# Storing the low parts of the projection weights in the first half of the sequence and loading them in the second

## The chip, the cores and the metric

The kernel runs on one core of a Trainium2 chip. The metric is the device time of one execution in microseconds (us). The engines are named as the profile names them: PE (TensorE, matrix products; PEld is its weight load), DVE (VectorE), ACT (ScalarE), POOL (GpSimd) and SP (SyncE, which here only issues DMAs; its instructions are listed as SPq). A DMA moves data between device memory and the on-chip memory.

## The reference

One layer of a decoder trunk over 1024 positions (`SEQ`) of 1024 channels (`D_MODEL`), all in float32:

```python
h = layer_norm(x, ln_in_g, ln_in_b)
u = h @ w_in            # conformer a, g | ssm z | ssm x, B, C | dt | gate_a | gate_b
y_a = silu(layer_norm(causal_dwconv31(a * sigmoid(g)))) @ w_conv_out
y_b = mamba2_ssd(z, x, B, C, dt) @ w_ssm_out      # conv4, chunks of 128, grouped RMS norm
mix = (sigmoid(gate_a) * y_a + sigmoid(gate_b) * y_b) @ w_o
h = layer_norm(2**0.25 * h + mix, ln1_g, ln1_b)
ffn = (silu(gate) * val) @ w_down  with  gate, val = split(causal_dwconv3(h @ w_up))
h = layer_norm(2**0.25 * h + ffn, ln2_g, ln2_b)
```

## The kernel before

**Halves.** The 1024 positions are worked in two halves of 512 (`hh` 0 and 1). Each half runs `ln_in` (norm and transpose), `mixers` (input projections, the state-space part in four groups, the 31-tap convolution) and `combine` (gates, `wssm`, `wconv`). Half 0 then runs `out_proj` with `wo`, half 1 `out_proj_pairs` inside `ffn_blocks`. The feed-forward part comes last, over all 1024 positions, from its own weights.

**Split products.** Every product is made of three matmuls (`mm3`, L166 to L168): a float32 operand is held as a high part in the fp32r type and a low part (what rounding left), and high·high, high·low and low·high are summed in PSUM. The helper `weights` makes the two parts of one weight tile of 128 x 1024: SP loads it into `st` (L152; three buffers), ACT casts it into `w[:, 0]` (L154), and DVE subtracts that from `st` into `w[:, 1]` (L155; for the first three tiles of half 0 POOL does it). `w` has three buffers too. The input projections, `wssm`, `wconv` and `wo` pass through it in both halves, from the same weights: `out_proj_pairs` reads each of the eight `wo` tiles twice, once for each pair of 128-position blocks.

**How long a tile lasts.** In most places one weight tile feeds 24 matmuls of 512 columns. In `out_proj_pairs` (L695) it feeds 12, since one pair of blocks is worked at a time.

**Order.** A scheduler orders each engine's instructions by a simulated time; `high_priority` moves the weight loads ahead. Each engine then runs its list in order. A DMA that waits for something on SP keeps all later DMAs of SP waiting. SP's DMAs also go round eight semaphores, so that one waits until the DMA eight before it has landed.

**Names around the change.** `st_c`, `st_z`, `st_ga`, `st_gg`, `st_so`, `st_gt`, `st_gb`, `st_sp`, `st_co`, `st_wo` are the staged weight tiles, `w_` the split ones; `c` is the accumulator of the 31-tap convolution (L420, on DVE); `x`, `in_g`, `in_b` are the rows and parameters of `ln_in`; `r`, `ln_g` (`ln1_g`), `ln_b` the rows and parameters of the norm behind `wo`; `h_scr`, `h1_scr`, `c_scr`, `g_scr`, `y_scr` are scratch in device memory.

Of the kernel before, what the change touches and what calls it, by code (L numbers as in the profile page):

```python
# [1 line left out]

# [6 lines left out]
F32 = mybir.dt.float32  # L9
# [7 lines left out]
P = 128  # L17
D = 1024
# [38 lines left out]
def kernel(  # L57
# [15 lines left out]
    V, A, G, TE, SY = nc.vector, nc.scalar, nc.gpsimd, nc.tensor, nc.sync  # L73
# [8 lines left out]
    dram = ctx.enter_context(tc.tile_pool(name="scr", bufs=1, space=DRAM))  # L82
# [5 lines left out]
    def bank(which):  # L88
        n_ps[0] += 1
        pl, tag = (pacc, "acc") if which else (psm, "sm")  # L90
        return pl.tile([P, 512], F32, tag=tag, name=f"{tag}{n_ps[0]}")
# [54 lines left out]
    g_scr = [dram.tile([8, P, HALF], F32, name=f"g_scr{i}") for i in range(2)]  # L146
    y_scr = [dram.tile([8, P, HALF], F32, name=f"y_scr{i}") for i in range(2)]

    def weights(src, name, pl=None, eng=None, bufs=None):
        with tc.high_priority(offset=4000):  # L150
            st = wst.tile([P, D], F32, tag="st", name=f"st_{name}")
            SY.dma_start(st, src)  # L152
            w = (pl or wsp).tile([P, 2, D], F32R, tag="w", bufs=bufs, name=f"w_{name}")
            A.copy(w[:, 0, :], st)  # L154
            (eng or V).tensor_tensor(  # L155
                out=w[:, 1, :], in0=st, in1=w[:, 0, :].bitcast(F32), op=ALU.subtract
            )
        return w

    def big_tile(name):  # L160
# [2 lines left out]
    def mm3(ps, wa, xa, start, stop, more=False):  # L163


        TE.matmul(ps, wa(0), xa(0), start=start, stop=False, skip_group_check=more)  # L166
        TE.matmul(ps, wa(0), xa(1), start=False, stop=False, skip_group_check=more)  # L167
        TE.matmul(ps, wa(1), xa(0), start=False, stop=stop, skip_group_check=more)  # L168
# [40 lines left out]
    def ln_stats(pl, tiles, name, sts=None):  # L209

        n = len(tiles)
        mv = pl.tile([P, n, 2], F32, tag="ln_mv", bufs=2, name=f"mv_{name}")
        rs = pl.tile([P, n], F32, tag="ln_rs", bufs=2, name=f"rs_{name}")
        for i, t in enumerate(tiles):
            if sts:
                st = sts[i]
            else:
                st = pl.tile([P, 2, 6], F32, tag="ln_st", bufs=2, name=f"st_{name}{i}")
                for q in range(2):
                    ln_part(pl, t, st, q)  # L220
            V.bn_aggr(out=mv[:, i, :], in_=st)
        A.activation(out=rs, in_=mv[:, :, 1], func=AF.Sqrt, bias=eps)
        V.reciprocal(out=rs, in_=rs)
        return mv, rs

    def ln_apply(t, mv, rs, i, g, b):
        V.scalar_tensor_tensor(
            out=t, in0=t, scalar=mv[:, i, 0:1], in1=g, op0=ALU.subtract, op1=ALU.mult
        )
        V.scalar_tensor_tensor(  # L230
            out=t, in0=t, scalar=rs[:, i : i + 1], in1=b, op0=ALU.mult, op1=ALU.add
        )
# [110 lines left out]
    def column(hh, hT, ct):  # L343
        ps = bank(1)
        project(ps, weights(wcol[ct], f"c{hh}_{ct}"), hT)
        return ps

    def first_columns(hh, hT, cts):

        ws = [weights(wcol[ct], f"c{hh}_{ct}", eng=None if hh else G) for ct in cts]  # L350
        pss = [bank(1) for _ in cts]
        for q in range(2):
            ts = slice(q * 256, (q + 1) * 256)
            for w, ps in zip(ws, pss):
                for n, (i, j) in enumerate(((0, 0), (1, 0), (0, 1))):
                    for k in range(KD):
                        TE.matmul(  # L357
                            ps[:, ts],
                            w[:, i, k * P : (k + 1) * P],
                            hT[:, j, k, ts],  # L360
                            start=n == 0 and k == 0,
                            stop=n == 2 and k == KD - 1,
                        )
        return pss
# [23 lines left out]
    def glu(pl, hh, hT, i):  # L388
        pa, pg = bank(1), bank(1)
        wa = weights(wcol[CT_A + i], f"ga{hh}_{i}")  # L390
        project(pa, wa, hT)
        wg = weights(wcol[CT_G + i], f"gg{hh}_{i}")
        project(pg, wg, hT)
        v = pl.tile([P, HALF + KC - 1], F32, tag="v", bufs=4, name=f"v{hh}_{i}")
        s = pl.tile([P, HALF], F32, tag="sig", name=f"sig{hh}_{i}")
        A.activation(out=s, in_=pg, func=AF.Sigmoid)
        A.copy(v[:, : KC - 1], v_halo[:, i, :])
        V.tensor_mul(v[:, KC - 1 :], pa, s)
        if hh == 0:
            A.copy(v_halo[:, i, :], v[:, HALF:])  # L400
        return v
# [293 lines left out]
    def out_proj_pairs(pl, rs, mixT, g, b, done):  # L695

        for t in range(4):
            SY.dma_start(rs[t], h_scr[1][t * P : (t + 1) * P, :])
        for pair in range(2):
            ts = (2 * pair, 2 * pair + 1)  # L700
            pss = {(t, q): bank(1) for t in ts for q in range(2)}
            for kp in range(4):
                for q in range(2):
                    w = weights(wo[q, kp], f"wo1_{pair}_{q}_{kp}")
                    for t in ts:
                        for k in range(2):
                            mm3(
                                pss[t, q],
                                lambda i: mixT[:, i, 2 * kp + k, t * P : (t + 1) * P],
                                lambda i: w[:, i, k * HALF : (k + 1) * HALF],  # L710
                                kp == 0 and k == 0,
                                kp == 3 and k == 1,
                            )
            for t in ts:
                for q in range(2):
                    r = rs[t][:, q * HALF : (q + 1) * HALF]
                    V.scalar_tensor_tensor(
                        out=r, in0=r, scalar=ALPHA, in1=pss[t, q], op0=ALU.mult, op1=ALU.add
                    )
            for t in ts:  # L720
                mv, rstd = ln_stats(pl, rs[t : t + 1], f"o1_{t}")
                ln_apply(rs[t], mv, rstd, 0, g, b)
                done(t)
# [20 lines left out]
    def ffn_blocks(tp, qp, mixT):  # L744
# [33 lines left out]
        def block_sums(t):  # L778
# [17 lines left out]
            if t >= 2:  # L796
# [5 lines left out]
                kept.clear()  # L802

        out_proj_pairs(tp, rest, mixT, g, b, block_sums)
        return {
            "b11": lambda i: b1[:, i, 0:4, :],
# [425 lines left out]
```

## Time and profile before

| | |
|---|---|
| median of 3 runs | 2033.85 us (2031.81 to 2035.5) |
| profiled execution: time, span | 2035.35 us, 2033.6 us |
| granted PE clock, mean | 0.991 |
| PE, DVE, ACT, POOL busy, share of the span | 97%, 84%, 49%, 8% |
| moved by DMA | 273.51 MB, mean 134 GB/s |
| device memory read, written | 222.36 MB, 49.55 MB |

The profile is one execution. Its time lies 1.75 us above its span. A row of the windows view gives, for a stretch of the span, the busy time of each engine with the number of its instructions, the granted PE clock (1.00 is full), the mean busy share of the 16 DMA engines, and what they moved in GB/s.

### The profile page before, as it was taken

What the parts mean: (1) busy time and instruction counts of PE and PEld (TensorE: products, weight loads), DVE (VectorE), ACT (ScalarE), POOL (GpSimd) and SP (SyncE); (2) the same over time, 40 slices, a digit from 0 to 9 for tenths busy, and PEclk for the clock granted to TensorE, in tenths of its full rate; (3) what the DMA queues carried; (4) which work ended last, traced back from release to release, by engine and by line L of the source; (5) the groups of instructions that cost most, each with busy time, mean ns of one, the idle gap of its engine ahead of it and who ended that gap; (6) DMA issues with size and microseconds to landing.
All of it is one profiled execution on the core that took longest, in us unless ns stands there. A gap on an engine that the chain in (4) does not pass through costs nothing.

```text
span 2033.6 us, 24571 instructions
## 1 busy us (share of the span) xinstructions
PE 1978.0 (97%) x9164; PEld 1628.0 (80%) x9164; DVE 1710.7 (84%) x2285; ACT 1001.8 (49%) x1448; POOL 171.9 (8%) x141
## 2 busy tenths in 40 slices
PE   6999999999999999999999999998899999989998
PEld 6888887888788888888888888887778888777886
DVE  7599999989766869999998976596998788777868
ACT  4465654556453356665454645364334445443432
POOL 2010101001400000100100130010000000010000
PEclk9999999999999999999999999999999999999999
DMA  6212233332546522222423354565342232377563
GB/s 219 93 63 94 79 102 106 99 104 101 174 133 216 195 88 77 88 85 75 127 86 107 109 166 138 188 234 202 130 153 106 99 109 99 109 258 264 175 224 109
DMA packets 97303, 273.51 MB, mean 134 GB/s; under 512 B 11168, under 2 KB 11168, under 8 KB 97184
## 3 DMA queue, kind: packets, MB, share of 16 engines
q1 hardware_dynamic: 87696, 242.06, 35.9%
q0 software_dynamic: 7184, 25.69, 3.3%
q10 hardware_dynamic: 2304, 4.20, 0.6%
q8 instruction: 72, 1.18, 0.2%
q14 instruction: 47, 0.39, 0.1%
HBM read 222.36 MB, written 49.55 MB: 134 GB/s over the span
## 4 chain that ended last, share of the span: by engine, by line
PE 66%; DVE 24%; DMA 4%; issue 4%; ACT 1%; SPq 0%; DVEq 0%; ACTq 0%
PE acc L166 17%; PE acc L168 17%; PE acc L167 17%; DVE c L420 8%; PE sm L166 3%; PE sm L167 3%; PE sm L168 3%; DVE xbc L375 2%; DMA dr<-b_scr 1%; PE acc L357 1%; PE sm L534 1%; DVE fo L895 1%; DMA st_wo<-wo 1%; PE sm L515 1%; DVE w_so L155 1%
## 5 line engine op out<-in xcount | busy, mean ns | idle before, releaser
L420 DVE SCALAR_TENSOR_TENSOR c<-v,pc,c 128x512 f32<-128x512 f32 x480 | 375.3, 805 | 7.6 <-ACT c L409 6.1
L478 POOL TENSOR_TENSOR au<-seg_mv,head_of 128x1024 fp32r<-128x1024 f32 x32 | 76.3, 2383 | 962.2 <-PE sm L487 730.4
L166 PE MATMUL acc<-hT,w_c 128*128 128x512 f32 x352 | 141.1, 401 | 0.0
L167 PE MATMUL acc<-hT,w_c 128*128 128x512 f32 x352 | 140.7, 400 | 0.0
L168 PE MATMUL acc<-hT,w_c 128*128 128x512 f32 x352 | 138.5, 393 | 0.0
L895 DVE SCALAR_TENSOR_TENSOR fo<-u,pc,fo 128x1024 f32<-128x1024 f32 x88 | 111.5, 1279 | 8.5 <-ACT fo L891 7.8
L375 DVE SCALAR_TENSOR_TENSOR xbc<-u,pc,xbc 128x512 f32<-128x512 f32 x144 | 109.7, 774 | 0.7 <-ACT xbc L373 0.5
L167 PE MATMUL acc<-w_z,hT 128*128 128x512 f32 x256 | 100.9, 394 | 0.0
L166 PE MATMUL acc<-w_z,hT 128*128 128x512 f32 x256 | 100.9, 401 | 0.0
L168 PE MATMUL acc<-w_z,hT 128*128 128x512 f32 x256 | 100.7, 396 | 0.0
L1021 ACT CAST w_dn<-dr 128x1024 fp32r<-128x1024 f32 (+1 forms) x73 | 60.8, 842 | 77.7 <-DVE dr L951 31.5
L154 ACT CAST w_c<-st_c 128x1024 fp32r<-128x1024 f32 x50 | 52.5, 1051 | 86.8 <-PE acc L168 66.1
L1022 DVE TENSOR_TENSOR w_dn<-dr,w_dn 128x1024 fp32r<-128x1024 f32 (+1 forms) x73 | 69.6, 963 | 17.6 <-ACT w_dn L1021 17.5
L167 PEld LDWEIGHTS acc<-hT,w_c 128*128 128x128 f32 x352 | 66.2, 188 | 16.8 <-issue 3.8
L168 PEld LDWEIGHTS acc<-hT,w_c 128*128 128x128 f32 x352 | 66.1, 188 | 16.0 <-issue 2.6
L166 PEld LDWEIGHTS acc<-hT,w_c 128*128 128x128 f32 x352 | 66.1, 188 | 15.9 <-issue 2.6
L155 DVE TENSOR_TENSOR w_c<-st_c,w_c 128x1024 fp32r<-128x1024 f32 x47 | 60.6, 1289 | 20.2 <-ACT w_c L154 20.2
L166 PE MATMUL acc<-h1s,w_s 128*128 128x512 f32 x168 | 66.6, 397 | 5.7 <-ACT u L875 5.7
L166 PE MATMUL acc<-h1b,w_ue 128*128 128x512 f32 x176 | 68.9, 392 | 2.6 <-ACT w_ue L740 1.4
L166 PE MATMUL sm<-h1b,w_s 128*128 128x512 f32 x176 | 70.3, 400 | 0.0
L167 PE MATMUL sm<-h1b,w_s 128*128 128x512 f32 x176 | 70.3, 399 | 0.0
L168 PE MATMUL sm<-h1b,w_s 128*128 128x512 f32 x176 | 69.9, 397 | 0.0
(352 smaller groups left out, 5811.1 us busy)
## 6 DMA issues: line engine op xcount, KB each, us to landing
st_c<-wcol SPq DMA_DIRECT2D x50, 512.0 KB, 3.5
st_z<-wz SPq DMA_DIRECT2D x32, 512.0 KB, 3.4
st_wo<-wo SPq DMA_DIRECT2D x24, 512.0 KB, 3.8
ra<-wup SPq DMA_DIRECT2D x22, 512.0 KB, 3.6
rb<-wup SPq DMA_DIRECT2D x22, 512.0 KB, 3.4
t_scr<-fo POOLq DMA_DIRECT2D x22, 512.0 KB, 4.2
dr<-t_scr SPq DMA_DIRECT2D x44, 256.0 KB, 3.4
dr<-wdown SPq DMA_DIRECT2D x38, 256.0 KB, 3.8
```

The source lines that it names most:

```text
L154: A.copy(w[:, 0, :], st)
L155: (eng or V).tensor_tensor(out=w[:, 1, :], in0=st, in1=w[:, 0, :].bitcast(F32), op=ALU.subtract)
L166: TE.matmul(ps, wa(0), xa(0), start=start, stop=False, skip_group_check=more)
L167: TE.matmul(ps, wa(0), xa(1), start=False, stop=False, skip_group_check=more)
L168: TE.matmul(ps, wa(1), xa(0), start=False, stop=stop, skip_group_check=more)
L357: TE.matmul(ps[:, ts], w[:, i, k * P : (k + 1) * P], hT[:, j, k, ts], start=n == 0 and k == 0, stop=n == 2 and k == KD - 1,)
L375: V.scalar_tensor_tensor(out=o, in0=u[:, k : k + HALF], scalar=pc[:, wc + k : wc + k + 1], in1=o, op0=ALU.mult, op1=ALU.add,)
L420: V.scalar_tensor_tensor(out=accs[i], in0=v[:, k : k + HALF], scalar=pc[:, wc + k : wc + k + 1], in1=accs[i], op0=ALU.mult, op1=ALU.add,)
L478: G.tensor_tensor(out=au, in0=seg_mv[:, c, :].unsqueeze(1).to_broadcast([P, 8, P]), in1=head_of[:, g, :].unsqueeze(2).to_broadcast([P, 8, P]),
L895: V.scalar_tensor_tensor(out=o, in0=u[:, k : k + T], scalar=pc[:, wc + k : wc + k + 1], in1=o, op0=ALU.mult, op1=ALU.add,)
L1021: A.copy(w[:, 0, cs], src)
L1022: V.tensor_tensor(out=w[:, 1, cs], in0=src, in1=w[:, 0, cs].bitcast(F32), op=ALU.subtract)
```

## The change

For each tile that `weights` makes in half 0 under a name with a 0 behind its letters (`c0_`, `ga0_`, `z0_`, `wo0_` and so on, 105 tiles), the low part is stored to device memory after it is made. For each such tile of half 1 (names with 1, and with 2 for the second pair of `out_proj_pairs`; 113 tiles) the low part is loaded into `w[:, 1]` in place of DVE's subtraction. ACT's cast and the load of `st` stay. All the new DMAs are issued by SP, 512 KB each.

```diff
+import re
...
+    low_scr = {}
+
     def weights(src, name, pl=None, eng=None, bufs=None):
+        half = re.match(r"([a-z]+)([012])_(.*)$", name)
+        key = half and (half.group(1), half.group(3))
         with tc.high_priority(offset=4000):
             st = wst.tile([P, D], F32, tag="st", name=f"st_{name}")
             SY.dma_start(st, src)
             w = (pl or wsp).tile([P, 2, D], F32R, tag="w", bufs=bufs, name=f"w_{name}")
+            if half and half.group(2) != "0" and key in low_scr:
+                SY.dma_start(w[:, 1, :].bitcast(F32), low_scr[key])
+                A.copy(w[:, 0, :], st)
+                return w
             A.copy(w[:, 0, :], st)
             (eng or V).tensor_tensor(
                 out=w[:, 1, :], in0=st, in1=w[:, 0, :].bitcast(F32), op=ALU.subtract
             )
+        if half and half.group(2) == "0":
+            low_scr[key] = dram.tile([P, D], F32, name=f"low_{name}")
+            SY.dma_start(low_scr[key], w[:, 1, :].bitcast(F32))
         return w
...
-                    w = weights(wo[q, kp], f"wo1_{pair}_{q}_{kp}")
+                    w = weights(wo[q, kp], f"wo{pair + 1}_{q}_{kp}")
```

The instruction lists show where the new DMAs stand. In a row, the name left of the arrow is written and the one right of it read. First SP's list at the start of `out_proj_pairs`, before:

```order
L152 DMA st_wo1_0_1_2_10548<-wo 128x1024
L203 DMA ln1_g_10370<-prow 128x1024
L203 DMA ln1_b_10372<-prow 128x1024
L750 DMA r0_10374<-h1_scr_125 128x1024
L750 DMA r1_10375<-h1_scr_125 128x1024
L152 DMA st_wo1_0_0_3_10565<-wo 128x1024
L750 DMA r2_10376<-h1_scr_125 128x1024
L152 DMA st_wo1_0_1_3_10582<-wo 128x1024
```

And SP's list at the same place after the change, where `low_wo0_q_kp` is the stored low part (L160 loads it):

```order
L157 DMA st_wo1_1_2_10758<-wo 128x1024
L160 DMA w_wo1_1_1_10726<-low_wo0_1_1_5649 128x1024
L215 DMA ln1_g_10580<-prow 128x1024
L215 DMA ln1_b_10582<-prow 128x1024
L157 DMA st_wo1_0_3_10775<-wo 128x1024
L762 DMA r0_10584<-h1_scr_125 128x1024
L762 DMA r1_10585<-h1_scr_125 128x1024
L160 DMA w_wo1_0_2_10743<-low_wo0_0_2_5544 128x1024
L762 DMA r2_10586<-h1_scr_125 128x1024
L157 DMA st_wo1_1_3_10792<-wo 128x1024
L160 DMA w_wo1_1_2_10760<-low_wo0_1_2_5680 128x1024
```

Each tile now takes two DMAs of 512 KB, and the low part of tile 0_2 stands behind the norm's parameters and two rows.

The second place is SP's list where half 0's `wo` meets the loads of half 1's `x`, before:

```order
L152 DMA st_wo0_0_3_5370<-wo 128x1024
L152 DMA st_wo0_1_0_5411<-wo 128x1024
L152 DMA st_wo0_1_1_5440<-wo 128x1024
L243 DMA x1_0_5147<-x 128x1024
L243 DMA x1_1_5149<-x 128x1024
```

And SP's list there after the change, where L169 stores a low part:

```order
L157 DMA st_wo0_0_3_5570<-wo 128x1024
L169 DMA low_wo0_0_0_5482<-w_wo0_0_0_5479 128x1024
L157 DMA st_wo0_1_0_5613<-wo 128x1024
L169 DMA low_wo0_0_1_5513<-w_wo0_0_1_5510 128x1024
L157 DMA st_wo0_1_1_5644<-wo 128x1024
L169 DMA low_wo0_0_2_5544<-w_wo0_0_2_5541 128x1024
L255 DMA x1_0_5341<-x 128x1024
L255 DMA x1_1_5343<-x 128x1024
```

One store now stands directly ahead of the four loads of `x`, and a store is placed behind the third load after its own tile's.

## The prediction

> **What bounds the kernel now.** I read the page's totals first, then the windows view by stage, since the change touches the second half of the sequence (640 to 1354 us) in one way and the first half in another.
>
> ```profile
> PE 1978.0 (97%) x9164; PEld 1628.0 (80%) x9164; DVE 1710.7 (84%) x2285; ACT 1001.8 (49%) x1448; POOL 171.9 (8%) x141
> ```
>
> ```profile
> 0.00:640.00 640.00, 622.00 (x2983) 514.13 (x2984) 548.89 (x752) 343.11 (x534) 70.24 (x45) 1.00 0.35 114
> 640.00:700.00 60.00, 58.01 (x307) 49.69 (x306) 47.88 (x73) 16.05 (x26) 0.00 (x0) 0.97 0.62 235
> 700.00:1303.00 603.00, 601.90 (x2849) 495.60 (x2848) 523.62 (x712) 324.52 (x477) 61.06 (x30) 1.00 0.34 109
> 1303.00:1354.00 51.00, 50.23 (x246) 41.77 (x245) 37.31 (x47) 29.32 (x41) 2.75 (x2) 1.00 0.78 278
> 1354.00:1400.00 46.00, 44.84 (x205) 36.70 (x204) 36.34 (x51) 24.97 (x43) 7.14 (x8) 1.00 0.58 204
> 1400.00:1510.00 110.00, 96.61 (x391) 76.65 (x390) 96.32 (x119) 40.23 (x42) 5.01 (x9) 0.94 0.42 144
> ```
>
> The first column after a stretch is its length, the second PE's busy time. From 700 to 1303 us, where nearly all removed work lies, PE is idle for 603.00 − 601.90 = 1.1 us. A busy PE may still run slowly, so the next row asks for its pace where nothing disturbs it.
>
> ```profile
> 1250.00:1300.00 50.00, 50.00 (x222) 41.42 (x222) 27.40 (x35) 14.37 (x18) 0.00 (x0) 1.00 0.47 145
> ```
>
> That is 222 matmuls in 50 us, 0.225 us each, with DVE busy little more than half. In the stages where DVE is full the instruction counts are higher only because short matmuls are among them; I see no slower pace. PE is therefore the bound of the affected half, and DVE's backlog is mostly the convolution, which fills DVE behind PE. What DVE saves cannot shorten PE's 602 us.
>
> **The change part by part.**
>
> *Removed: 113 subtractions on DVE.* The view of L155 over this half gives their count (the row of the waits they carry) and what one costs.
>
> ```profile
> L155 DVEq EVENT_SEMAPHORE  x113: 21/21/50, 690.2 to 1352.5; - x113
> ...
> L155 DVE TENSOR_TENSOR w_z<-st_z,w_z x16: 1206/1217/1225, 721.3 to 1076.7; 128x1024 fp32r<-128x1024 f32 x16
> ...
> L155 DVE TENSOR_TENSOR w_wo<-st_wo,w_wo x16: 1209/1222/1226, 1294.0 to 1345.9; 128x1024 fp32r<-128x1024 f32 x16
> ```
>
> 113 x 1.22 us is about 138 us of DVE. Their cover is PE, so they are worth at most PE's idle time in the stretches where they lie: 1.1 us up to 1303 and 51.00 − 50.23 = 0.8 us up to 1354. Part of that has other causes (the list of PE's waits below). I take −1.0 us; the ends are 0 and −1.9.
>
> *Kept on ACT and for `st`.* The cast stays. The load of `st` for the third tile ahead now waits for the cast and no longer for DVE, which is earlier: nothing lost.
>
> *Added in the second half: 113 loads of 512 KB,* each into a `w` buffer, so each waits until PE is done with the tile three before. A normal tile lasts 24 x 0.225 = 5.4 us, so the load has 10.8 us until PE wants it. What such a load takes:
>
> ```profile
> st_z<-wz SPq DMA_DIRECT2D x32, 512.0 KB, 3.4
> ```
>
> With 3.4 us there remain 7.4 us of slack, and the DMA engines are a third busy in this stretch (0.34). The extra 113 − 16 = 97 loads there are 51 MB in 603 us, 84 GB/s more on 109. Hidden by PE: 0.
>
> *Added in `out_proj_pairs`* (1303 to 1354). Here a tile lasts 12 x 0.225 = 2.7 us and the stretch is already full of transfers.
>
> ```profile
> DMA packets 3892, 14.20 MB, mean 278 GB/s; under 512 B 432, under 2 KB 432, under 8 KB 3889
> ...
> q1 hardware_dynamic: 3889, 14.16, 77.8%
> ...
> 1310.00:1315.00 5.00, 5.00 (x24) 4.15 (x23) 2.45 (x2) 1.10 (x2) 0.00 (x0) 1.00 0.99 374
> 1315.00:1320.00 5.00, 5.00 (x32) 4.38 (x31) 0.40 (x1) 1.47 (x3) 0.00 (x0) 1.00 1.03 408
> ```
>
> The first two rows are the DMA view of that stretch; in the last two the DMA engines are full (0.99 and 1.03) at 374 and 408 GB/s. Of 16 low loads the first two are issued before it; 14 x 0.524 = 7.3 MB come on top of 14.2, 21.5 MB in all. Bounds: with the engines never idle at 408 GB/s they take 52.7 us, +1.7 us. At the rate at which they worked per busy time here (14.16 MB in 0.778 x 51 = 39.7 us, 357 GB/s) 60.2 us, +9.2. Between them I follow the queue. SP's list puts `ln_g`, `ln_b`, a staged tile, two rows and then the low part of tile 0_2 behind the low part of tile 1_1, which can go when the first tile is done, at 1303.3 + 2.7 = 1306.0. The issue times of before show that burst:
>
> ```profile
> 1306.46 0.43 SPq L203 DMA_DIRECT2D ln_g<-prow  x1
> 1306.94 0.42 SPq L203 DMA_DIRECT2D ln_b<-prow  x1
> 1307.40 0.98 SPq L750 DMA_DIRECT2D r<-h_scr  x2
> 1308.61 0.33 SPq L152 DMA_DIRECT2D st_wo<-wo  x1
> ```
>
> Seven transfers at 0.524 MB / 408 GB/s = 1.28 us, and 2.1 us of latency (3.4 − 1.28), land the low part of tile 0_2 at 1306.0 + 9.0 + 2.1 = 1317.1. PE wants it after 52 matmuls (11.7 us) and 16 transposes, whose time the chain of waits gives:
>
> ```profile
> 1346.75 1.75 PE sm L758 x16
> ```
>
> That is 1303.3 + 11.7 + 1.75 = 1316.8: just on time. Behind it 30 more transfers stand up to the low part of the last tile, 38.4 us, so that one lands at 1355.5 with ten matmuls (2.3 us) still to run, 1357.8. PE alone, with 204 matmuls (45.9 us) and 48 transposes (5.25 us) up to the same point, would be through at 1354.5. That is +3.3 us with DMA engines that never wait. They will wait a little: each low load waits for PE, SP keeps everything behind it, and two stores of finished rows (`h1_scr` from `r4`, `r5`) now stand ahead of the low parts of the second pair's last tiles. I add a third, +4.5 us in all, between 1.7 and 9.2.
>
> The Trainium skill's page "DMA: Bandwidth & Descriptors" (section Specifications) gives about 358 GB/s as the limit of device memory for one core; by it the 21.5 MB take 60 us, an estimate, +9 us. The trace goes above it, with 408 GB/s over 5 us, so I keep that rule for the range's upper side only.
>
> *Added in the first half: 105 stores of 512 KB,* 55 MB over 640 us, 86 GB/s on 114. A store stands behind the load that already waited for the same subtraction, so SP waits no longer than before. The new wait is a cast that needs its buffer's old store landed; PE's use of that buffer (5.4 us and more) covers it. At one place a store sits on a chain: where half 1's `x` is loaded.
>
> ```profile
> 641.18 1.91 SPq L243 DMA_DIRECT2D x<-x  x4
> ...
> 647.27 1.29 DVE L207 BATCH_NORM_STATS2 st_in<-x 128x6 f32<-128x512 f32 x2 [5.90 <-DMA x<-x]
> ...
> PE sm L192 <- DVE x L230: 1.1, 1, 1.1
> PE acc L166 <- DVE r L687: 0.9, 1, 0.9
> ...
> 642.00:666.00 24.00, 22.01 (x102) 18.02 (x101) 18.73 (x30) 8.53 (x13) 0.00 (x0) 0.96 0.99 384
> ```
>
> DVE sat 5.9 us for `x`, then is full, and PE waits for its norm (L230) near 660. The DMA engines are at 0.99 there. One store ahead is 1.28 us, two would be 2.6, none 0: I take +1.3 us, since one stands directly in front.
>
> *Scheduling.* State-space steps stand earlier in PE's list of half 1, because the scheduler sees a freer DVE. PE has no idle time there to win; 0, with ±1.
>
> **Sum.** −1.0 + 4.5 + 1.3 = +4.8 us, say +5. The profiled execution (2035.35 us, its span plus 1.75) becomes 2040.4; it lies 1.5 us above the median, 2033.85, so the forecast for the median is 2038.9, a rise of 0.25%. Bounds of the terms: −1.9 + 1.7 + 0 = −0.2 and 0 + 9.2 + 2.6 = +11.8. A change under 0.2% (4.1 us) is about what this measurement cannot tell from none; the three runs alone spread 3.7.
>
> **The rivals.**
>
> *Hidden anyway, no measurable change (0.29).* The DMA engines stay fed, at 408 GB/s: −1.0 + 1.7 + 0 to 1.3, some +1 to +2, 2035.5. For it: the low part of 0_2 is forecast to arrive on time. Against it: the engines must be full for 50 us, while SP waits in order.
>
> *Faster (0.12).* DVE's relief reaches PE through the norm stretch and what follows. It needs more than half of what there is: 2.0 us idle from 640 to 700, and its clock of 0.97 over 60 us, 1.8 us; 1.1 and 0.8 after that; and some of the 13.4 us from 1400 to 1510, where DVE is 96.3 of 110 us busy and its list is slightly reordered. Taking all 5.7 before 1354 with no DMA cost gives 2028; −5, 2029, is the case I carry. It decides if the transfers of `out_proj_pairs` stay below PE's time. Against it: no subtraction is removed after 1354, and nothing in the first half.
>
> *SP's order stalls the middle (0.12).* A low load has 7.4 us of slack, and it stands in one list with stores that wait for ACT and DVE.
>
> ```profile
> SPq L558 <- ACT ya L557: 22.9, 5, 11.6
> SPq L429 <- DVE c L420: 18.7, 7, 5.7
> ```
>
> The longest wait (11.6 us, between 690 and 1300) passes 7.4 by 4.2 us. If three or four such waits fall badly, +13 with the forecast's +5: 2052. Against it: most of these waits are for PE's own product and so end when the buffer does.
>
> *PE's clock.* A longer pause costs more than itself. Three rows show how long one has to be:
>
> ```profile
> 1330.00:1335.00 5.00, 4.22 (x18) 3.24 (x18) 4.63 (x7) 3.06 (x4) 0.00 (x0) 1.00 0.70 255
> ...
> 1400.00:1405.00 5.00, 0.54 (x3) 0.11 (x1) 2.79 (x5) 2.06 (x4) 0.00 (x0) 0.99 0.78 262
> 1405.00:1410.00 5.00, 4.16 (x10) 3.30 (x11) 5.00 (x7) 2.79 (x3) 0.00 (x0) 0.50 0.80 279
> ```
>
> A pause under 1 us leaves the clock at 1.00; one of over 4 us is followed by 5 us at 0.50, in which about ten matmuls fewer run, 2.3 us. My stalls are of 1 to 2 us each, so this is not in the sum; where stalls meet in one pause of that length it adds 2.3, 2041, inside the forecast's range. The Trainium skill's "TensorE: Matmul & The Clock Gate" (Part 1) puts the length at about 3.4 us; these rows agree, with under 1 and over 4 on either side.
>
> **How the numbers follow.** Forecast (+4.1 to +12, likeliest 2039): 0.47. With the third rival, slower 0.59; same 0.29; faster 0.12. The forecast's own range is 2038 to 2046. The range for 8 in 10 reaches from 2031 (part of the faster case and half a microsecond below the lower sum) to 2050 (the upper sum, 2045.7, and part of the third rival).
>
> **What the new profile would show.** DVE's L155 is down by 113 in half 1 and the 700 to 1303 row still has PE idle for 1 to 2 us: step one holds. The 1303 to 1354 stretch, measured from the first `w_wo` matmul to the last, is 4 to 5 us longer, its DMA share near 0.95, and PE's waits there name `low` loads: step two. `x` lands a microsecond later and PE's pause near 660 grows: step three. The forecast fails if the pairs' stretch keeps its length, if PE waits on low loads in the mixers, or if the feed-forward stages (no change in their work) move by more than 2 us.

## The result, and the profile after

| | before | after |
|---|---|---|
| median of the runs made together, 4 each | 2034.67 us (2031.81 to 2036.94) | 2045.41 us (2043.39 to 2048.82) |
| ratio after : before, 95% interval | | 1.0055 (1.0036 to 1.0075) |
| profiled execution: time, span | 2035.35, 2033.6 us | 2043.39, 2041.7 us |

The change makes the kernel slower by 0.55%; the interval corresponds to 7 to 15 us. The forecast had the sign and the place, and about half of the size.

The page's totals of the kernel after:

```profile
PE 1979.8 (97%) x9164; PEld 1627.9 (80%) x9164; DVE 1585.2 (78%) x2172; ACT 1002.5 (49%) x1448; POOL 163.9 (8%) x141
```

DVE lost 113 instructions (2285 to 2172) and 125 us of work, and PE's busy time did not move (1978.0 before). The windows view says where PE stood. The columns are those of the prediction's rows.

```profile
690.00:1298.00 608.00, 607.97 (x2903) 501.66 (x2902) 424.94 (x625) 326.03 (x480) 54.05 (x30) 1.00 0.59 193
1298.00:1362.00 64.00, 56.18 (x259) 45.35 (x258) 31.44 (x46) 33.35 (x46) 5.93 (x4) 0.97 0.92 343
...
1305.00:1310.00 5.00, 5.00 (x24) 4.06 (x22) 0.00 (x0) 1.42 (x2) 0.00 (x0) 1.00 1.01 356
1310.00:1315.00 5.00, 1.67 (x10) 1.40 (x9) 0.00 (x0) 1.52 (x2) 0.00 (x0) 0.89 1.02 413
1315.00:1320.00 5.00, 5.00 (x24) 4.40 (x23) 2.77 (x4) 4.12 (x9) 0.00 (x0) 0.77 1.03 410
1320.00:1325.00 5.00, 5.00 (x27) 4.25 (x26) 1.29 (x2) 3.86 (x6) 0.00 (x0) 1.00 1.02 408
1325.00:1330.00 5.00, 2.80 (x17) 2.21 (x17) 2.46 (x4) 3.15 (x5) 0.00 (x0) 1.00 1.03 410
```

In the middle of half 1 the DMA engines' share rose from 0.34 to 0.59 and PE is idle for 0.03 us of 608: the loads are hidden, and the 1.1 us of idle time that was there is gone. In `out_proj_pairs` (1298 to 1362) PE is idle for 7.8 us of 64 at a mean clock of 0.97, with DMA engines full from 1305 to 1335. The length of that stretch is read from its first matmul on `w_wo` to the first matmul on `h1s`, the next stage's input; the rows give the first and the last start of each group. Before:

```profile
L166 PE MATMUL acc<-w_wo,mixT x64: 387/389/502, 1303.3 to 1352.7; 128*128 128x512 f32 x64
...
L166 PE MATMUL sm<-h1s,w_s x33: 387/390/794, 1405.8 to 1447.1; 128*128 128x512 f32 x33
```

And after:

```profile
L178 PE MATMUL acc<-w_wo,mixT x64: 388/389/505, 1298.4 to 1360.6; 128*128 128x512 f32 x64
...
L178 PE MATMUL sm<-h1s,w_s x28: 387/389/796, 1410.8 to 1446.5; 128*128 128x512 f32 x28
```

The stretch grew from 1405.8 − 1303.3 = 102.5 us to 1410.8 − 1298.4 = 112.4. In the profiled executions everything ahead of it came 4.9 us earlier, and from the first `h1s` matmul to the end of the span it took 3.1 us longer (627.8 to 630.9). Sum: −4.9 + 9.9 + 3.1 = +8.1, the difference of the spans. Not all of the −4.9 is the change's doing: the kernel before plus 16 stores (below), whose work ahead of the stretch is that of the kernel before, starts it at 1300.2, 3.1 us earlier than the profile of before. PE's waits in 1290 to 1390 (in total, times, longest, us), before:

```profile
PE acc L166 <- ACT w_wo L154: 0.8, 1, 0.8
```

And after:

```profile
PE sm L770 <- DMA r<-h_scr: 3.3, 1, 3.3
PE acc L178 <- ACT h1raw L785: 2.2, 1, 2.2
PE acc L179 <- DMA w_wo<-low_wo: 1.6, 2, 0.8
PE acc L178 <- DVE r L729: 0.6, 1, 0.6
```

They sum to 7.7 us. Only 1.6 us of it is for the loaded low parts. The longest is for row `r0`, an old transfer. The second is for a PSUM bank that ACT has still to copy out (`h1raw`, a transposed row). That `r0` was late is not its cause: it is 2.2 us too in the kernel with the rows on POOL's queue (below), where PE does not wait for `r0`. The DMA view of 1298 to 1362:

```profile
DMA packets 6008, 21.94 MB, mean 343 GB/s; under 512 B 661, under 2 KB 661, under 8 KB 6004
...
w_wo<-low_wo SPq DMA_DIRECT2D x14, 512.0 KB, 7.8
st_wo<-wo SPq DMA_DIRECT2D x11, 512.0 KB, 8.7
r<-h_scr SPq DMA_DIRECT2D x8, 512.0 KB, 9.4
```

A staged tile here took 8.7 us from issue to landing (median), where one in the middle of half 1 took 3.4 before the change.

### The profile page after: what moved, and what is told of

Its sections match the earlier page's. It is cut to its first block, busy times and chain, and to the rows that moved or that the text cites. A ratio compares the mean times of both kernels' runs of the same rounds, so it can differ in the third digit from the quotient of the medians.

```text
span 2041.7 us, 24792 instructions
## 1 busy us (share of the span) xinstructions
PE 1979.8 (97%) x9164; PEld 1627.9 (80%) x9164; DVE 1585.2 (78%) x2172; ACT 1002.5 (49%) x1448; POOL 163.9 (8%) x141
## 4 chain that ended last, share of the span: by engine, by line
PE 77%; DVE 15%; DMA 5%; issue 2%; ACT 1%; SPq 0%; DVEq 0%; ACTq 0%
PE acc L178 19%; PE acc L180 19%; PE acc L179 19%; DVE c L432 4%; PE sm L178 4%; PE sm L179 4%; PE sm L180 4%; PE sm L546 2%; PE acc L369 1%; DVE xbc L387 1%; PE sm L527 1%; DMA dr<-b_scr 1%; PE sm L535 1%; PE sm L204 1%; DMA c_scr<-c 1%
## 5 line engine op out<-in xcount | busy, mean ns | idle before, releaser
L178 PE MATMUL acc<-h1b,w_ue 128*128 128x512 f32 x176 | 68.9, 391 | 2.6 <-ACT w_ue L752 1.4
L179 PE MATMUL acc<-h1b,w_ue 128*128 128x512 f32 x176 | 68.5, 389 | 0.0
L507 ACT ACTIVATE m<-sm 128x512 f32<-128x512 f32 x64 | 37.3, 595 | 63.4 <-PE sm L499 63.3
```

The source lines that it names most:

```text
L507: A.activation(out=mq, in_=pg, func=AF.Relu)
```

## The experiments

Two theories of the loss stood at first. A1: the added transfers come as a burst at the start of the first pair, where the engines were full already, and the rows wait behind them. A2: each load costs about the same wherever it stands. For each kernel the table gives the median, its ratio to the kernel before run beside it, and the stretch of its profiled execution, worked out as above; each ran 5 to 11 times. The stretch is that of one execution, and the profiled one lay up to 5.1 us from its kernel's median (2050.14 against 2045.0 for the low parts on POOL's queue), so the ratio is the firmer of the two.

| kernel | median, us | ratio (95%) | stretch, us |
|---|---|---|---|
| everything but `wo` | 2034.4 | 0.9997 (0.9987 to 1.0006) | 102.5 |
| `wo` alone | 2046.62 | 1.0062 (1.0048 to 1.0077) | 111.7 |
| stores alone | 2034.79 | 1.0003 (0.9994 to 1.0012) | 102.7 |
| second pair alone loads `wo` | 2037.15 | 1.0017 (1.0008 to 1.0026) | 108.3 |
| first pair alone loads `wo` | 2047.05 | 1.0062 (1.0050 to 1.0074) | 113.3 |
| rows on POOL's queue | 2043.36 | 1.0048 (1.0036 to 1.0060) | 111.2 |
| kernel before plus 16 stores | 2045.83 | 1.0063 (1.0049 to 1.0077) | 116.3 |
| low parts on POOL's queue | 2045.0 | 1.0063 (1.0051 to 1.0075) | 119.0 |
| half of each low part | 2043.96 | 1.0044 (1.0031 to 1.0058) | 110.4 |
| a quarter of each low part | 2041.79 | 1.0034 (1.0021 to 1.0047) | 108.8 |
| transposes put back | 2044.93 | 1.0051 (1.0038 to 1.0065) | 112.8 |
| kernel before, transposes early | 2035.11 | 1.0001 (0.9991 to 1.0010) | 102.9 |

Beside the first four the kernel before had 2033.19 us, beside the next four 2033.76, beside the last two pairs 2034.22 and 2034.78. None of these versions beats it.

**Everything but `wo`, and `wo` alone.**

```diff
-        key = half and (half.group(1), half.group(3))
+        key = half and half.group(1) != "wo" and (half.group(1), half.group(3))
...
-        if half and half.group(2) == "0":
+        if key and half.group(2) == "0":
```

The other kernel has `== "wo"` in the first place.

> The change without wo: its eight tiles are neither stored nor loaded, the subtraction stays there; the other 97 tiles are stored and loaded. Theory A (the whole loss is the pairs' stretch of half 1, which went from 102.5 us to 112.5 us between its first matmul and the first of the feed-forward part; all else gains or costs little): that stretch is back at 102 to 104 us, and the time is 0 to 5 us below the kernel before. Theory B (the doubled DMA traffic costs a little everywhere, so that the median rose 10.7 us where the profiled run rose 8.0): the pairs' stretch is back, but the time stays 2 to 6 us above the kernel before.

> Only wo's eight tiles are stored and loaded (16 loads); all else subtracts as before. Theory A: the pairs' stretch takes 111 to 114 us and the time is 9 to 12 us above the kernel before, about the full change's loss. Theory B: the stretch is as long, but the time is only 6 to 8 us above, the rest of the loss being elsewhere.

The whole loss is `wo`'s: alone it gives 1.0062, the other 97 loads and their stores give 0.9997, between −2.6 and +1.2 us. So the earlier start seen in the profiles (the first `w_wo` matmul of `out_proj_pairs` also comes 3.8 us earlier in the kernel without `wo`) is not a gain that the medians confirm, and 3.1 us of it came without any change to the work, as said above.

**Stores alone.**

```diff
-            if half and half.group(2) != "0" and key in low_scr:
+            if False:
```

> All 105 stores of half 0 stay, nothing is loaded back; half 1 subtracts as before. Theory A: the stores are hidden, within 2 us of the kernel before, and x lands at most 1.5 us later. Theory B: 2 to 4 us above.

1.0003, and the stretch at 102.7: 55 MB of stores cost nothing that can be measured.

**One pair alone.**

```diff
-            if half and half.group(2) != "0" and key in low_scr:
+            if half and half.group(2) != "0" and key in low_scr and not name.startswith("wo1"):
```

The other kernel has `"wo2"`, so that the first pair loads and the second subtracts.

> The full change, but the first pair of out_proj_pairs subtracts and only the second pair loads low parts (8 of the 16). Theory A1 (a burst: the rows and norm parameters of the first pair meet the low loads, and rows and low parts queue behind each other): nearly all of the 10 us of that stretch is won back, 103 to 106 us, and the time is within 3 us of the kernel before. Theory A2 (each low load there costs alike, 16 at 0.6 us): half is won back, the stretch takes 107 to 108 us, and the time is 4 to 6 us above.

> All of the change, except that the second pair of out_proj_pairs makes its low parts on DVE as before; the first pair's eight tiles load them. Stretch from the first w_wo matmul to the first up_rest matmul: 102.5 us before, about 112 with all sixteen loads. Theory A1 (what costs is the burst of transfers at the start of the first pair, behind which the rows r0 to r3 wait; PE's pause there is 3.3 us, its clock falls after it, and the ACT copies are late): nearly all of the loss is here, stretch 109 to 112, median 2040 to 2044. Theory A2 (each low load costs about 0.6 us wherever it stands): half of the loss, stretch 107 to 108, median 2038 to 2040. The second pair's loads alone gave 108.3 and 2037.15; if both halves cost, their sum should be near the full loss of +9 to +10.

The first pair's eight loads cost as much as all sixteen (1.0062), the second pair's eight 0.17%. So the costs are unequal, against A2, and the first pair is the place, as A1 says. But neither theory gave both kernels: the second pair alone came out about as A2 had it (108.3 us against 107 to 108, and 4.0 us above in the medians against 4 to 6), outside A1's range, and the first pair alone lost more than A1's range. By the medians the two together are more than the whole (0.79% against 0.55%), though the intervals allow a plain sum. That PE, once late, has more time for what comes next would explain it; it is not shown. With the second pair alone the waits of PE are others again, one of them for the norm of `r4`:

```profile
PE sm L770 <- DVE r L242: 2.3, 1, 2.3
PE acc L179 <- DMA w_wo<-low_wo: 2.0, 1, 2.0
```

**Queue or bytes.** Is it the order of SP's queue that makes `r0` late (theory Q), or full DMA engines whatever the queue (theory B)? Two kernels take transfers off SP's queue.

```diff
-            SY.dma_start(rows[t], h1_scr[t * P : (t + 1) * P, :])
+            G.dma_start(rows[t], h1_scr[t * P : (t + 1) * P, :])
```

```diff
-                SY.dma_start(w[:, 1, :].bitcast(F32), low_scr[key])
+                (G if key[0] == "wo" else SY).dma_start(w[:, 1, :].bitcast(F32), low_scr[key])
```

> The whole change, with the rows r0 to r3 that are transposed during the first pair loaded from POOL's queue instead of SP's, so that they no longer stand behind the low part of tile 1_1 and the staged tiles; the bytes are the same. Theory Q (the order of SP's queue makes the rows late): the 3.3 us wait of PE for r goes, its clock stays near 1.00 in 1310 to 1320, the stretch falls from 112.5 to 105 to 108 us, median 2037 to 2041. Theory B (the DMA engines are full, and it does not matter which queue asks): the rows land as late or something else does by as much, stretch 110 to 113, median 2043 to 2046.

> The whole change, with the sixteen low parts of wo loaded from POOL's queue instead of SP's; SP's list in the stretch is then that of before, and a low load that waits for its buffer holds up only POOL. Theory Q (order and head-of-line waiting in SP's queue): rows land as before, the stretch is 103 to 106 us, median 2034 to 2038. Theory B (full DMA engines): stretch 109 to 113, median 2041 to 2046, with PE's waits perhaps on other tiles. If this or the rows on POOL's queue were faster than before the change by more than 0.2%, it would be the better version; I expect neither.

With the rows on POOL's queue PE no longer waits for `r`, and waits for low parts instead. Its waits in 1290 to 1390:

```profile
PE acc L179 <- DMA w_wo<-low_wo: 4.1, 4, 2.2
PE acc L178 <- ACT h1raw L785: 2.2, 1, 2.2
PE acc L178 <- DVE r L729: 0.3, 1, 0.3
```

With the low parts on POOL's queue they are late for longer:

```profile
PE acc L179 <- DMA w_wo<-low_wo: 7.2, 3, 4.4
PE acc L178 <- ACT h1raw L785: 2.2, 1, 2.2
PE sm L770 <- ACT h1raw L785: 1.5, 2, 0.8
```

Both ratios stay in the interval of the change. Q fell as the account of the loss: the queue decides which tile is late (with the rows on POOL's queue `r0` is in time), and the loss stays.

**The bytes without the dependence.** The kernel before, with each of the sixteen low parts also stored, and nobody to read them:

```diff
                     w = weights(wo[q, kp], f"wo1_{pair}_{q}_{kp}")
+                    SY.dma_start(
+                        dram.tile([P, D], F32, name=f"low{pair}_{q}_{kp}"),
+                        w[:, 1, :].bitcast(F32),
+                    )
```

> The kernel before, with one extra thing: in out_proj_pairs each of the sixteen low parts that DVE makes is also stored to its own place in device memory (512 KB each, 8.4 MB, issued by SP), and nobody reads it. The bytes of that stretch are those of the change, but PE waits for no low part to arrive. Theory B (bytes on full DMA engines and SP's queue behind them make the rows and staged tiles late): stretch 108 to 113 us, median 2040 to 2045. Theory D (PE's dependence on the loaded low parts is what costs): stretch within 2 us of 102.5, median within 2 us of before.

```profile
PE acc L167 <- DVE w_wo L155: 3.6, 3, 2.4
PE acc L166 <- DVE r L721: 3.1, 1, 3.1
PE acc L166 <- ACT w_wo L154: 1.2, 1, 1.2
```

PE waits for no new transfer itself, and no low part is loaded, yet the loss is the same, 1.0063. So D fell: sixteen more transfers of 512 KB in this stretch are enough, in either direction. The kernel doesn't isolate the bytes, though. ACT can't cast the next tile into a `w` buffer until the store from that buffer has landed, and DVE, and PE behind it, follow ACT. The waits of ACT in 1290 to 1362:

```profile
ACT w_wo L154 <- DMA low<-w_wo: 4.5, 3, 1.8
```

Each store also makes SP wait for DVE, which the low parts on POOL's queue exclude from their side. A kernel that adds the bytes here and lets nothing wait for them was not run.

**Fewer bytes in each load.** Of `wo`'s low parts only the first `n` columns are loaded, and DVE subtracts for the rest; `n` is 512, then 256.

```diff
-                SY.dma_start(w[:, 1, :].bitcast(F32), low_scr[key])
+                n = HALF if key[0] == "wo" else D
+                SY.dma_start(w[:, 1, :n].bitcast(F32), low_scr[key][:, :n])
                 A.copy(w[:, 0, :], st)
+                if n < D:
+                    V.tensor_tensor(
+                        out=w[:, 1, n:], in0=st[:, n:], in1=w[:, 0, n:].bitcast(F32), op=ALU.subtract
+                    )
```

> The whole change, except that for each wo tile of the second half only the first 512 of the 1024 columns of the low part are loaded (256 KB) and DVE subtracts for the other 512. Same number of loads, same places in SP's queue, same dependence of PE on them; half the added bytes in the pairs' stretch. Theory B (bytes on full DMA engines): about half of the loss, stretch 106 to 109 us against 102.5 and 112.5, median 2037.5 to 2041. Rival N (each load costs by its place in the queue and the wait that it adds, whatever its size): stretch 110 us or more, median 2042 to 2046. If the loss depends on a threshold of bytes (the rows just in time or not), the stretch is within 2 us of 102.5 and the median within 2 us of before.

> As the kernel with half of the low part loaded, with a quarter: 256 columns (128 KB) per wo tile, DVE subtracts for the other 768. Theory B in proportion to the bytes: a quarter of the loss, stretch 104 to 106 us, median 2035.5 to 2038. Rival N (each load by its place and its wait): stretch 110 us or more, median 2042 to 2046. With a threshold of bytes: stretch within 1 us of 102.5 and no measurable change of the median.

The median loss falls with the bytes (0.55, 0.44 and 0.34%, with intervals that overlap), but not in proportion: a quarter of them still costs 6.3 us of the stretch and 0.34%. B in proportion missed both kernels. The rival (each load by its place and its wait, whatever its size) had both numbers of the half right (110.4 us, 2043.96) and forecast a little more than the quarter cost (108.8, 2041.79). So much of the loss does not go by the bytes. That it comes with the number of transfers is not shown, since DVE subtracts again in both kernels. PE's waits with a quarter are many small ones:

```profile
PE acc L184 <- DVE ts L808: 1.7, 1, 1.7
PE sm L775 <- DMA r<-h_scr: 1.3, 1, 1.3
PE acc L184 <- DMA w_wo<-low_wo: 0.6, 1, 0.6
PE acc L183 <- DVE r L734: 0.6, 1, 0.6
```

**Is it PE's own order?** In all versions that load in the first pair, the scheduler put the transposes of `r0` behind 52 matmuls of the pair and not behind 62 (theory O: PE asks for `r0` 2.3 us too soon, whatever the bytes). One kernel has the whole change with the transposes put back, the other the kernel before with `r0`'s behind 50 and `r1`'s behind 60.

```diff
+                    if pair == 0 and (kp, q) in ((2, 0), (3, 0)):
+                        with tc.issue_after(ins.ins if hasattr(ins, "ins") else ins):
+                            between(kp - 2)
```

Here `ins` is the last matmul of a tile and `between` does the transposes of two rows and what follows them, moved here from ahead of `out_proj_pairs`. In the second kernel `issue_after` holds the matmuls of tile 0_2 (queued behind the last transpose of `r1`) instead.

> The whole change, with the transposes of the rows r0 and r1 put back in PE's list to where they stood before the change (behind 62 matmuls of the first pair instead of 52), those of r2 behind 86. Bytes and loads are those of the change. A quarter of the added bytes cost 6.3 us of the stretch, half 7.9 and all 10.0, so about 5 us do not go by bytes. Theory O (that part is PE's own list, which the scheduler reordered so that it asks for r0 ten matmuls, 2.3 us, sooner than it can land): the wait for r shrinks from 3.3 to about 1 us or none, no halved clock after it, stretch 105 to 108 us against 112.5, median 2037 to 2040.5. Theory B alone (bytes on full DMA engines): another tile is late instead, stretch 110 to 113, median 2043 to 2046.

> The kernel before, without any store or load of a low part, with the transposes of r0 forced into PE's list behind 50 matmuls of the first pair and those of r1 behind 60 (both behind 62 before). No byte is added. Theory O: r0 is late for this place, PE waits 1 to 3 us for r, stretch 104 to 107 us against 102.5, median 2035 to 2038. Theory B alone: without added bytes the rows are there in time, stretch within 1 us of 102.5, no measurable change.

O fell on both sides. With no byte added, `r0` is in time for the earlier place, but for 0.2 us. PE's waits of the kernel before with early transposes:

```profile
PE acc L168 <- DVE w_ue L155: 0.8, 1, 0.8
PE sm L761 <- DMA r<-h_scr: 0.2, 1, 0.2
```

With the change and the old place, PE runs on past `r0` and stops for the low part of tile 0_2. The timeline of PE and the windows of that kernel:

```profile
1317.51 0.79 PE L179 MATMUL acc<-w_wo,mixT 128*128 128x512 f32 x1 [5.37 <-DMA w_wo<-low_wo]
```

```profile
1300.00:1305.00 5.00, 5.00 (x24) 4.14 (x23) 2.07 (x3) 2.73 (x3) 0.00 (x0) 1.00 0.67 211
1305.00:1310.00 5.00, 5.00 (x24) 4.14 (x23) 0.00 (x0) 2.10 (x2) 0.00 (x0) 1.00 0.95 317
1310.00:1315.00 5.00, 2.13 (x10) 1.44 (x8) 0.00 (x0) 1.04 (x1) 0.00 (x0) 0.91 1.02 411
1315.00:1320.00 5.00, 2.49 (x6) 2.01 (x7) 0.00 (x0) 0.00 (x0) 0.00 (x0) 0.50 1.03 410
```

A wait of 3.3 us for one tile became a wait of 5.4 us for another. Four orders of the same bytes (the change, rows on POOL's queue, low parts on POOL's queue, transposes put back) lose 0.5 to 0.6% each; what differs is mainly the tile that PE waits for. The wait of 2.2 us for `h1raw` is gone too with the transposes put back, and one of 3.0 us for a row's norm has come, so PE's list does decide which waits there are, but not the sum.

**What stays open.** Shown are the place (`wo`'s loads, those of the first pair above all) and that tiles land late there while the DMA engines are full. Why a quarter of the bytes costs more than half of the loss isn't settled. PE's dependence on the loaded parts, SP's queue and the transposes' place are each excluded as the sole cause; the number of transfers against their bytes, DVE, which subtracts again in the kernels with a half and a quarter, and the rest of the reordered lists were not tried apart. One measurement bears on it: over the 25 us that begin some 4.6 us behind the first `w_wo` matmul the DMA engines are busy for 0.93 before the change, for 1.00 with a quarter and for 1.02 with the whole (341, 361 and 395 GB/s). There was little room, and a quarter already took it; that this is the reason is not shown.

## Why the prediction was right or wrong

*113 subtractions removed, −1.0 us: held in the profile.* From 690 us to `out_proj_pairs`, PE's idle time fell from 1.1 us to 0.03. From 680 to 1298 us it is 0.03 in the kernel without `wo` too, and 0.56 in the kernel before plus 16 stores, which subtracts there. The medians can't show it: 0.9997 has ±2 us.

*97 low loads hidden, 0: right.* PE waits for none of them.

*One store ahead of `x`, +1.3 us: the transfer was right, the cost wrong.* DVE begins on `x` at 647.5 us, against 647.27 before, although SP issued the load 1.1 us earlier (640.1 against 641.2). The kernel after:

```profile
L219 DVE BATCH_NORM_STATS2 st_in<-x x8: 675/676/698, 647.5 to 653.2; 128x6 f32<-128x512 f32 x8
L255 SPq DMA_DIRECT2D x<-x x4: 423/512/1431, 640.1 to 642.7; - x4
...
PE sm L204 <- DVE x L242: 0.7, 1, 0.7
```

From issue to DVE's start it is 7.4 us against 6.1, the 1.3 longer that was forecast. But PE's wait for the norm did not grow with it: 0.7 us against 1.1. Nor did it shrink by the change: it is 0.6 and 1.2 us in the two kernels whose work here is that of before (plus 16 stores; transposes early), and 0.9 with the stores alone. The load was issued sooner in this profile, which the step left out, and the stores alone cost nothing (1.0003).

*`out_proj_pairs`, +4.5 us between 1.7 and 9.2: mechanism and place right, size wrong.* The bytes (21.5 MB forecast, 21.94 over 64 us measured) and the engines' rate were right. The profile gives +9.9 us for the stretch, 7.8 − 0.8 = 7.0 of it new idle time, and about 64 x 0.03 = 1.9 lost to the clock; `wo` alone measures +12.6 us (9.8 to 15.7). The range held partly by luck: its upper side was made of transfers at 357 GB/s and 2.6 us for `x`, but the engines ran at 405 to 417 GB/s while they were full, and `x` cost nothing. Three steps failed.

- I followed one tile, low 0_2, and called it "just on time". My own queue has `r0` as the fifth transfer behind 1306.0, 11.2 us after the first `w_wo` matmul (2.7 + 5 x 1.28 + 2.1), and PE's new list asks for it at 11.7. I never worked out that margin of half a microsecond. It landed at 1313.63 − 1298.4 = 15.2.
- The landing of low 0_2, forecast at 1317.1 − 1303.3 = 13.8 us, is shown by the kernel with the transposes put back: 1317.51 − 1300.2 = 17.3, which is 3.5 us later. I counted seven transfers from the burst's start at 408 GB/s, as if the engines were empty before it and took transfers one after the other. By the four rows above they moved (211 + 317 + 411) x 5 us + 410 x 2.5 us = 5.7 MB from 1300 to that landing, 10.9 transfers of 0.524 MB. The list holds nine up to low 0_2, with the two that were still under way at the start (low 0_1 and the staged tile 1_2). So transfers that stand behind it in the list had their share by then; that they are served side by side is inferred from this count.
- I kept the clock out of the sum, because a stall of 1 to 2 us seemed harmless. The stalls met in one of 3.3 us, and the clock fell to 0.89 and 0.77. My own row of 642 to 666 us should have warned me: the clock is 0.96 there with PE idle for 2.0 us in all, in pauses of 1.1 and 0.9.

The Trainium skill's "DMA: Bandwidth & Descriptors" (Specifications) would have given +9 us by its limit of about 358 GB/s, an estimate. That is near the measured loss, though not by its reason: while they were full the engines ran at 405 to 417 GB/s, and PE's loss came from what was late and not from the total.

*Scheduling, 0 ±1.* The reordered transposes alone cost nothing measurable (1.0001).

*What the profile should have shown.* L155 down by 113: yes. PE idle for 1 to 2 us from 700 to 1303: no, 0.03. First to last `w_wo` matmul 4 to 5 us longer: no, 62.2 us against 49.4, 12.8 longer. PE's waits naming `low` loads: partly, 1.6 of 7.7 us. The DMA share near 0.95: 0.92. `x` a microsecond later and a longer pause near 660: no. Feed-forward stages within 2 us: no, 3.1 us in the profiled execution. In the experiments that part (627.8 us before) takes 625.8 to 629.2 where the stretch kept its length and 629.0 to 634.2 where it grew; what links the two no run shows.

*The rivals.* "Hidden anyway" assumed engines that are always fed and a tile that is on time; the engines were fed, and tiles were late all the same. "SP's order stalls the middle" didn't happen. "Faster" didn't either; the kernel without `wo`, its best case, is at 0.9997.

## What to carry to other kernels

Where a stage's DMA engines are full even for 10 us, work out the landing of every tile that the bound engine needs there, the old ones too; the one that an added transfer makes late need not be the added one, and in four orders tried here reordering only changed which it is. A busy engine that isn't the bound (DVE at 84%) can be relieved of 125 us and give nothing, and transfers put where the DMA engines are a third busy cost nothing that could be measured here; so apply such a trade only where there is bandwidth, and even there measure whether it buys anything. Upper bounds made of bytes over a rate leave out the clock.

## What the runs showed of the hardware that was not expected

**Pauses that lower the clock can be short.** My rows of before had under 1 and over 4 us, but its pauses of 1.1 and 0.9 us near 660 already lowered it:

```profile
660.00:665.00 5.00, 3.01 (x19) 2.36 (x18) 5.00 (x8) 3.32 (x6) 0.00 (x0) 0.92 1.03 415
665.00:670.00 5.00, 5.00 (x18) 4.00 (x17) 5.00 (x9) 0.00 (x0) 0.00 (x0) 0.73 0.51 211
```

In the kernel before with early transposes the same two waits (1.2 and 0.9 us) left it at 1.00:

```profile
660.00:665.00 5.00, 3.82 (x25) 2.98 (x23) 5.00 (x7) 2.01 (x5) 0.00 (x0) 1.00 1.02 408
665.00:670.00 5.00, 4.17 (x18) 3.49 (x19) 5.00 (x11) 1.60 (x3) 0.00 (x0) 1.00 0.62 254
```

With `wo` alone, PE's wait for `r` of 2.6 us was followed by 0.66 over 5 us; with the second pair alone, the wait of 2.0 us for a low part (in the first row) was, too:

```profile
1345.00:1350.00 5.00, 2.95 (x13) 2.15 (x12) 1.81 (x3) 1.68 (x3) 1.28 (x1) 1.00 1.02 408
1350.00:1355.00 5.00, 5.00 (x16) 3.95 (x16) 3.69 (x6) 1.05 (x1) 0.00 (x0) 0.66 0.56 212
```

With the transposes put back, a later wait of 3.0 us left it at 1.00:

```profile
1335.00:1340.00 5.00, 2.04 (x12) 1.48 (x12) 4.11 (x7) 3.57 (x6) 0.00 (x0) 1.00 1.03 411
1340.00:1345.00 5.00, 5.00 (x25) 4.17 (x24) 4.79 (x9) 2.95 (x5) 1.30 (x1) 1.00 0.87 329
```

So the length of a pause alone doesn't decide, and a clock lost near 660 in one execution and not in another is part of the scatter of these profiles. The Trainium skill's "TensorE: Matmul & The Clock Gate" (Part 1) says about 3.4 us of idle time, seen through a window that runs freely; the scatter fits such a window, the pauses of 2.0 us and less are shorter than its figure.

**A transfer's landing time depends on all that is under way.** The median of the staged `wo` tiles is 3.9 us over 1298 to 1362 before (the row here) and 8.7 after (its row stands above), with the same size and queue:

```profile
st_wo<-wo SPq DMA_DIRECT2D x12, 512.0 KB, 3.9
```
